# A gating stage whose first product is split into seven half-size products, and whose layer norm is applied behind the mixing

## The chip, the core and the metric

The program runs on one core of a Trainium2 chip. The core has a matrix engine (PE, whose weight loads are listed apart as PEld), a vector engine (DVE), a scalar engine (ACT), a third elementwise engine (POOL) and a sequencer (SP) that here only starts transfers. Each engine takes its instructions strictly in the order of its own list, and a wait at the head of a list holds back everything behind it. Transfers are started by SP or by POOL; only those of POOL add to what already stands at their target. The metric is the device time of one execution in microseconds (us), the median of several runs of one kernel.

## The reference

Two decoder layers work on 512 tokens of width 1024. Each layer has a mixer and an MLP, and each is fed by an RMS norm that is shifted and scaled by vectors made from a conditioning vector. Layer 0 mixes by pooling; layer 1 mixes by the gating stage, which this document is about:

```python
def layernorm(x, g, b):
    mu = jnp.mean(x, axis=-1, keepdims=True)
    xc = x - mu
    var = jnp.mean(xc * xc, axis=-1, keepdims=True)
    return xc * lax.rsqrt(var + LN_EPS) * g + b

def sgu_mixer(h, w_in, ln_g, ln_b, w_s, b_s, w_out):      # h: 1, 512, 1024
    z = jax.nn.gelu(h @ w_in, approximate=False)          # w_in: 1024, 2048
    u, v = jnp.split(z, 2, axis=-1)                       # the u half and the v half
    v = layernorm(v, ln_g, ln_b)
    v = v.reshape(B_, 4, 128, 8, 128)                     # chunks of 128 tokens, 8 heads of 128 channels
    ws = jnp.where(tril, w_s, 0)                          # w_s: 8, 128, 128
    mixed = jnp.einsum('hts,bnshc->bnthc', ws, v) + b_s.T[None, None, :, :, None]
    return (u * mixed.reshape(B_, S_, 1024)) @ w_out
```

## The kernel before

Every large product is made three times over: both operands are split into a high part (a rounded copy, made by ACT, line 201: `wh`) and a low part (the difference, made by DVE, line 202: `wl`), and `mm3` (line 214) adds low x high, high x low and high x high in PSUM. Activations have the same two parts: `hb` is the normed and modulated input, four tiles of two 128-channel blocks each, with hi and lo.

The first MLP ends with products in four chunks; the last of them, labelled `(3, 4)`, multiplies an activation tile `o` (hi by ACT line 680, lo by DVE line 681) with two weight tiles `bt`. Its 24 matmuls carry line 214 and the tile name `pm`; the rest of that MLP's matmuls are on line 976. Around it stands `normed(0, 1, 0)` (tokens 0 to 255) and, within the first v product, `normed(1, 1, 0)` (tokens 256 to 511): a reciprocal root on POOL (`rr`, line 281), a scaled copy of x (`xs`), 16 transposes on PE (`px`, line 1145), scale and shift (line 1152 on DVE, line 1150 on ACT), and the split into `hb`.

The gating stage before, in the order of PE:

1. The v product: two column halves x two halves of the tokens, 48 matmuls of 128x512 for each of these four pieces (`po<-wh,hb`), evicted by a GELU on ACT (line 1272).
2. The layer norm of v, on DVE: statistics (lines 1277, 1279), a small root on POOL, one pass for mean and root (line 1281), then two passes of 128x1024 for `ln_g` and `ln_b` per token tile (line 1283), whose rows were loaded to all partitions (`lnt`).
3. The u product by heads, `do_u(n)`: 8 input blocks x 3 = 24 matmuls of 128x512 for each of 8 heads (`po<-hb,wh`), GELU on ACT (line 1304). The weights lie in four plain loads of 1 MB (`ur`).
4. The mixing by heads, `do_mix(hd)`: four small products on PE (line 1312) into a PSUM bank, `b_s` added (line 1314), times u (line 1315), split for the last product (lines 1319, 1320). A string gives the order `u0 u1 u2 u3 m0 u4 m1 m2 u5 m3 m4 u6 m5 u7 m6 m7`.
5. The product with `w_out` (`po<-wh,gt`).

Between these, `ex` holds 24 small jobs that make columns of the conditioning vectors (`ada`, line 238 on DVE: one 512 KB load and one 128x1024 pass each) and one job, `spread_cols`, that turns a column into a row on all partitions by way of DRAM (`line`, `gainm`, `gb`).

PE's list is in program order. In this part of the program the lists of the other engines are made by the scheduler of the framework: it takes what is ready by its own estimate of time, and by the order of the program among what is ready. It, too, assigns buffers: the weight splits have five pairs, the pool of raw loads (`w4`) three buffers.

The MLPs already use the scheme that the change brings to u: `s_units` makes a quarter of the hidden layer by seven products of half the size, with sums of activations (the class `Sums`, whose passes are on lines 676, 705 and 706) and sums of weights. Sums of weights are made by transfers from POOL that add onto a tile (line 822).

## Time and profile before

| | |
|---|---|
| Time of the kernel, median of 3 runs | 836.05 us (835.79 to 836.57) |
| Time of the profiled execution | 835.0 us |
| Its span | 833.3 us |
| Instructions in it | 12670 |
| Mean granted TensorE clock | 0.998 |
| Transfers | 190.72 MB, 229 GB/s in the mean |

A span runs from the first to the last instruction that the profile holds; the time of the execution is 1.7 us more. Times within the program are us from the start of the span. A group row of the profile reads: line, engine, operation, output<-inputs by the program's names, shapes, x count, then busy us and mean ns of one. A timeline row reads: start, us, engine, line, operation, names, x count, and in square brackets how long the engine had been idle and what ended it. Matmuls overlap, so what one costs is read from the distance of starts and not from the length of one. DVE and ACT overlap a little too: a 128x1024 pass of DVE is listed with 1.22 us and the next one starts 1.14 us after it.

### The profile page before, as it was taken

To read this page: it belongs to the slowest core of one execution; us is meant where nothing else is said; L and a number is where in the kernel's file an instruction comes from. 1 tells how busy PE (TensorE), PEld (TensorE's weight loads), DVE (VectorE), ACT (ScalarE), POOL (GpSimd) and SP (SyncE) were. 2 spreads that over 40 slices of the span, in tenths; PEclk is the share of its full clock that TensorE was granted. 3 is DMA by queue.
4 is the path that set the end of the run, shared out by engine and by line. 5 is a ranking of instruction groups with operands and counts; after the bars stand their busy time and mean duration, and the time that the engine had idled before them with its cause. 6 is when DMAs were issued, how large, how long until landed. Compare 5 with 4: busy or idle time off the path is not lost.

```text
span 833.3 us, 12670 instructions
## 1 busy us (share of the span) xinstructions
PE 821.1 (99%) x4866; PEld 724.7 (87%) x4866; DVE 683.4 (82%) x882; ACT 506.3 (61%) x721; POOL 118.0 (14%) x140
## 2 busy tenths in 40 slices
PE   9999999999999999999999999999999999999996
PEld 6878899999888888888888888999999988888885
DVE  6999899998789868797898768795887678976887
ACT  3286777866756655676333237876776766565562
POOL 3010010000223200020110002100001032321000
PEclk9999999999999999999999999999999999999999
DMA  9999879999999989464757848865888799998502
GB/s 360 407 364 336 293 155 288 289 278 265 292 227 200 204 226 248 145 250 148 255 180 250 273 135 282 223 178 127 233 266 209 205 229 238 193 217 223 161 17 85
DMA packets 52227, 190.72 MB, mean 229 GB/s; under 512 B 5803, under 2 KB 5955, under 8 KB 51142
## 3 DMA queue, kind: packets, MB, share of 16 engines
q1 hardware_dynamic: 36944, 133.45, 44.3%
q0 software_dynamic: 14928, 56.12, 34.7%
q8 instruction: 38, 0.62, 0.3%
q10 hardware_dynamic: 294, 0.34, 0.1%
q14 instruction: 23, 0.19, 0.1%
HBM read 183.58 MB, written 6.30 MB: 228 GB/s over the span
## 4 chain that ended last, share of the span: by engine, by line
PE 82%; DVE 8%; DMA 5%; issue 2%; ACT 2%; POOL 0%; POOLq 0%; DVEq 0%; ACTq 0%
PE pm L976 28%; PE po L214 17%; PE b211q L214 3%; PE b315q L976 2%; PE b305q L976 2%; PE b201q L214 2%; PE b111q L214 2%; PE b205q L214 2%; DVE wl L202 2%; PE b101q L214 2%; PE b215q L214 2%; PE b301q L214 2%; DMA bt<-in_w 1%; DMA ada<-in_ada 1%; PE b011q L214 1%
## 5 line engine op out<-in xcount | busy, mean ns | idle before, releaser
L976 PE MATMUL pm<-wh,o 128*128 128x512 f32 x736 | 182.4, 390 | 0.5 <-DVE o L681 0.5
L976 PEld LDWEIGHTS pm<-wh,o 128*128 128x128 f32 x736 | 137.7, 188 | 29.5 <-DVE o L681 0.9
L976 PE MATMUL pm<-wl,o 128*128 128x512 f32 x368 | 98.4, 389 | 0.0
L201 ACT ACTIVATE wh<-bt 128x1024 fp32r<-128x1024 f32 x64 | 66.9, 1057 | 44.9 <-PE pm L976 33.7
L202 DVE TENSOR_TENSOR wl<-bt,wh 128x1024 fp32r<-128x1024 f32 x64 | 77.5, 1219 | 14.6 <-ACT wh L201 14.6
L976 PEld LDWEIGHTS pm<-wl,o 128*128 128x128 f32 x368 | 69.1, 188 | 14.4
L238 DVE SCALAR_TENSOR_TENSOR ada<-ada,cb 128x1024 f32<-128x1024 f32 x56 | 68.0, 1218 | 11.3 <-DMA ada<-in_ada 11.1
L681 DVE TENSOR_TENSOR o<-g,o 128x1024 fp32r<-128x1024 f32 x56 | 68.2, 1218 | 6.2 <-ACT o L680 6.2
L680 ACT ACTIVATE o<-g 128x1024 fp32r<-128x1024 f32 x56 | 58.6, 1048 | 10.1 <-PE pm L976 7.3
L214 PE MATMUL po<-hb,wh 128*128 128x512 f32 x208 | 64.1, 389 | 0.0
L201 ACT ACTIVATE wh<-raw 128x1024 fp32r<-128x1024 f32 x35 | 37.0, 1058 | 33.6 <-PE pm L976 13.5
L201 ACT ACTIVATE wh<-b 128x1024 fp32r<-128x1024 f32 x32 | 34.0, 1062 | 37.6 <-PE pm L976 31.4
L955 POOL DMA_DIRECT2D bt<-in_w x48 | 41.8, 906 | 104.9 <-DVE wl L202 104.8
L202 DVE TENSOR_TENSOR wl<-b,wh 128x1024 fp32r<-128x1024 f32 x32 | 39.2, 1224 | 21.3 <-ACT wh L201 21.3
L202 DVE TENSOR_TENSOR wl<-raw,wh 128x1024 fp32r<-128x1024 f32 x35 | 42.5, 1220 | 12.8 <-ACT wh L201 12.7
L214 PEld LDWEIGHTS po<-hb,wh 128*128 128x128 f32 x208 | 39.1, 188 | 7.9
L737 ACT ACTIVATE g<-g 128x512 f32<-128x512 f32 (+1 forms) x72 | 40.5, 579 | 1.1
L214 PE MATMUL po<-hb,wl 128*128 128x512 f32 x104 | 40.9, 393 | 0.0
L214 PE MATMUL po<-wh,gt 128*128 128x512 f32 x128 | 40.0, 391 | 0.0
L214 PE MATMUL po<-wh,hb 128*128 128x512 f32 x128 | 39.9, 390 | 0.0
L214 PEld LDWEIGHTS po<-wh,gt 128*128 128x128 f32 x128 | 24.0, 188 | 5.2 <-DVE gt L1320 0.2
L214 PEld LDWEIGHTS po<-wh,hb 128*128 128x128 f32 x128 | 24.0, 188 | 5.1
(469 smaller groups left out, 2096.6 us busy)
## 6 DMA issues: line engine op xcount, KB each, us to landing
ada<-in_ada SPq DMA_DIRECT2D x74, 512.0 KB, 5.2
bt<-in_w POOLq DMA_DIRECT2D x48, 512.0 KB, 10.1
bt<-in_w SPq DMA_DIRECT2D x16, 512.0 KB, 6.4
raw<-in_w SPq DMA_DIRECT2D x16, 512.0 KB, 6.9
b<-in_w SPq DMA_DIRECT2D x16, 512.0 KB, 4.8
b<-in_w POOLq DMA_DIRECT2D x16, 512.0 KB, 10.2
wh<-in_ada SPq DMA_DIRECT2D x8, 512.0 KB, 9.4
wl<-in_ada SPq DMA_DIRECT2D x8, 512.0 KB, 9.9
```

The costliest lines, as they stand in the source:

```text
L201: A.activation(h[:, c], r[:, c], AF.Copy)
L202: V.tensor_tensor(l[:, c], r[:, c], f32(h[:, c]), ALU.subtract)
L214: T.matmul(o[:, c], a, b[:, c], start=first and q == 0 and not c.start, stop=last and q == 2 and c.stop is None, **kw)
L238: keep(V.scalar_tensor_tensor(r, r, 1.0, cb, ALU.mult, ALU.mult, accum_out=pmv[i, b][:, j : j + 1]))
L680: A.activation(o[0], a, AF.Copy)
L681: V.tensor_tensor(o[1], a, f32(o[0]), ALU.subtract)
L737: A.activation(t, t, AF.Square)
L955: G.dma_start(r, piece(c, *nxt, q), accum_op=ALU.add)
L976: T.matmul(banks[hf], o[a][:, 2 * q + p, hf], w[q][b][:, S * p : S * p + S], start=start and q + n + p == 0, stop=stop and q + n + p == 4, ...
```

## The change

The u half of the first product is no longer made by heads but by two groups `j` of 512 channels. A group has four weight blocks of 512 x 256 (`w_u[j, r, n]`, r the half of the inputs, n the half of the columns), and seven products of 24 matmuls of 128x256. Products 1, 5, 6 and 4 use one weight tile (`ua[:, j]`) to which POOL's transfers add a further block each time the tile has been split; products 3 and 7 use `ub`, product 2 a raw load. The activation side needs sums of the normed input, so `normed` now keeps it in full precision (`h32`, in the slots S4 and S6) instead of in a two-buffer scratch tile (`tt`). Products 1, 6, 7, 4 add up in one PSUM bank, 5 and 3 in a second, 2 in a third that starts as a copy of the first.

The layer norm keeps only mean and root ahead of the mixing, in one pass on ACT. `ln_g` multiplies the mixed result (a number per partition, since channels lie on partitions there). For `ln_b` the sums over the rows of the masked `w_s` are made from a second load of it (`nat`), spread over the partitions, multiplied by `ln_b` and added to `b_s` (`row_sums`).

The order string, the places of the `ex` jobs and the order in which the last product takes its heads change as well.

```diff
-POPS = (3, 3, 3, 2, 2, 1, 1, 1)
...
+            h32[:] = [slot(t, [P, 4, S], "h32") for t in ("S4", "S6")]
...
-            tt = h32[k // 4][:, k % 4 : k % 4 + 2, c] if i and n else sm.tile([P, 2, 256], F32, name="tt", tag="tmp", bufs=2)
+            tt = h32[k // 4][:, k % 4 : k % 4 + 2, c] if i else sm.tile([P, 2, 256], F32, name="tt", tag="tmp", bufs=2)
...
+    lnc = sm.tile([P, LINE], F32, name="lnc", tag="lnc", bufs=1)
+    nc.sync.dma_start(lnc[:, 0 : 2 * HEADS], lnp)
+    rc = lnc[:, 2 * HEADS : 3 * HEADS]
+    ua, ub = (slot(t, [P, 2, D], "ur") for t in ("S5", "S7"))
+
+    def u_add(t, j, r, n):
+        G.dma_start(t, w_u[j, r, n], accum_op=ALU.add)
...
+    ALLU = [(0, m) for m in (1, 5, 2, 6, 3, 7)] + [(1, 1), (0, 4)] + [(1, m) for m in (5, 2, 6, 3, 7, 4)]
+    def u_prep(j, m):
+        if m == 2:
+            t = raw4(w_u[j, 1, 0])
+        else:
+            t = ub[:, m // 7] if m in (3, 7) else ua[:, j]
+        wu[j, m] = split(t, 1, RESET if m == 1 else UNDER)
+        if m in CHAIN_U:
+            u_add(t, j, *CHAIN_U[m])
+        elif j == 0 and m == 3:
+            nc.sync.dma_start(t, w_u[1, 1, 1])
+        elif j == 0 and m == 7:
+            nc.sync.dma_start(t, w_u[1, 0, 1])
+            u_add(t, 1, 1, 1)
+    CHAIN_U = {1: (0, 1), 5: (1, 1), 6: (1, 0)}
...
+        if m in (1, 5):
+            banks[j] = four[j] if m == 1 else bank(f"u{j}{m}q")
...
+        for f in range(2):
+            for k in range(4):
+                mm3(po[:, f], cut(wv, ALL, k, slice(P * f, P * f + P)), us_.of[m](k), m in (1, 5) and f + k == 0, m in (4, 3, 2) and f + k == 4, skip_group_check=True)
+        r, n = TAKES[m]
+        with tc.high_priority():
+            if m == 1:
+                WU[j] = seeded(full_u, f"u{j}2q", w[0])
+                A.activation(WU[j], XU[j], AF.Copy)
+                return
+            t = u_tile(j, n)[:, :, 256 * r : 256 * r + 256]
+            if m in (5, 6):
+                A.activation(t, po, AF.Copy)
+            elif m in (2, 4):
+                A.activation(t, po, AF.Gelu)
+            else:
+                V.tensor_tensor(t, *((po, t) if m == 3 else (t, po)), ALU.subtract)
+                A.activation(t, t, AF.Gelu)
...
+    def do_mix(hd):
+        po = mixed[hd] = four[(2, 3, 2, 3, 3, 2, 0, 2)[hd]]
...
+        V.scalar_tensor_tensor(o, o, lnc[:, hd : hd + 1], b, ALU.mult, ALU.add)
+        finish(hd)
+
+    def row_sums():
+        for hd in range(HEADS):
+            w = nat[:, P * hd : P * hd + P]
+            A.activation(w, w, AF.Copy, accum_out=rc[:, hd : hd + 1])
+        spread_cols(rc, "rows")
+        for hd in range(HEADS):
+            V.scalar_tensor_tensor(wb[1][:, hd], gbs[0][:, P * hd : P * hd + P], lnc[:, HEADS + hd : HEADS + hd + 1], wb[1][:, hd], ALU.mult, ALU.add)
...
-        V.tensor_scalar(v, v, ag[:, 0:1], r, ALU.subtract, ALU.mult)
-        for n, op in ((0, ALU.mult), (1, ALU.add)):
-            V.tensor_tensor(v, v, lnt[n].rearrange("p (a b) -> p a b", a=2), op)
+        V.scalar_tensor_tensor(m, ag[:, 0:1], -1.0, r, ALU.mult, ALU.mult)
+        A.activation(v, v, AF.Identity, bias=m, scale=r)
...
-    for op in "u0 u1 u2 u3 m0 u4 m1 m2 u5 m3 m4 u6 m5 u7 m6 m7".split():
+    for op in "u u u u m2 u m3 u u m0 m1 u u u m6 u m7 u u m4 u".split():
```

`finish(hd)`, called when both the mixing and u of a head are there, multiplies the two out of the PSUM bank and splits the product. In the lists that follow a number behind a name tells buffers apart, and the waits are those on DVE, ACT (Activation), PE, transfers of SP (DMAHW) and transfers of POOL (DMASW).

**At the end of the first MLP, on DVE.** `o_3531` (now `o_3529`) is the activation tile of the MLP's last product, its weight splits are `wl_3535` and `wl_3539` (now `wl_3533` and `wl_3537`), and the rows of `tt` or `h32` and `hb` are `normed(0, 1, 0)`. Before:

```order
L1152 TENSOR_SCALAR tt_3487<-px_3482,scl10_92,mods1_89 128x256
L1152 TENSOR_SCALAR tt_3497<-px_3492,scl10_92,mods1_89 128x256
L681 TENSOR_TENSOR o_3531<-g_1778,o_3531 128x1024
L202 TENSOR_TENSOR wl_3535<-bt_2496,wh_3534 128x1024
L681 TENSOR_TENSOR hb_3478<-tt_3487,hb_3478 128x2x256
L681 TENSOR_TENSOR hb_3479<-tt_3497,hb_3479 128x2x256
```

Now, from the fourth of the four scale-and-shift rows on:

```order
L1151 TENSOR_SCALAR h32_3479<-px_3511,scl10_92,mods1_89 128x256
L1080 TENSOR_TENSOR tmp_3520<-y_2775,gb_2697 128x512
L679 TENSOR_TENSOR hb_3480<-h32_3478,hb_3480 128x2x256
L1081 TENSOR_TENSOR x1_3298<-x1_3298,tmp_3520 128x512
L1080 TENSOR_TENSOR tmp_3525<-y_2775,gb_2697 128x512
L679 TENSOR_TENSOR hb_3481<-h32_3478,hb_3481 128x2x256
L679 TENSOR_TENSOR hb_3482<-h32_3479,hb_3482 128x2x256
L1081 TENSOR_TENSOR x1_3298<-x1_3298,tmp_3525 128x512
L679 TENSOR_TENSOR hb_3483<-h32_3479,hb_3483 128x2x256
L679 TENSOR_TENSOR o_3529<-g_1778,o_3529 128x1024
L200 TENSOR_TENSOR wl_3533<-bt_2496,wh_3532 128x1024
L200 TENSOR_TENSOR wl_3537<-bt_2497,wh_3536 128x1024
```

The low part of the MLP's last operand stood behind two scale-and-shift rows; it now stands behind four of them and eight passes of 128x512.

**In the u product, on ACT.** Before, the high parts of u's weights (`wh<-ur`) and the GELUs, with waits on plain loads:

```order
L201 ACTIVATE wh_4064<-ur_4062 128x1024 [waits DMAHW0_49,DVE_49]
L1304 ACTIVATE u_3963<-po_3982 128x512 [waits PE_49]
L201 ACTIVATE wh_4110<-ur_4062 128x1024 [waits DVE_49]
L1304 ACTIVATE u_3963<-po_4024 128x512 [waits PE_49]
L201 ACTIVATE wh_4161<-ur_4159 128x1024 [waits DMAHW1_49,DVE_49]
```

Now, with `wh_4093` the weights of product (0, 6), `wh_4125` those of (0, 3), `v_3601` the layer norm's pass over the last two token tiles, and `u02q` the PSUM bank in which product (0, 2) adds up:

```order
L199 ACTIVATE wh_4093<-ur_3598 128x1024 [waits DMASW4_49]
L199 ACTIVATE wh_4125<-ur_3599 128x1024
L1366 ACTIVATE v_3601<-v_3601,lnc_3596,rr_4031 128x1024 [waits DVE_49,Activation_49]
L1308 ACTIVATE u02q_4090<-po_4062 128x512 [waits PE_49]
L1366 ACTIVATE v_3601<-v_3601,lnc_3596,rr_4042 128x1024 [waits DVE_49,Activation_49]
```

The copy into `u02q`, without which product (0, 2) can't start, stands three rows behind a split that waits for a transfer of POOL.

**At the mixing, on DVE.** Before, around the mixing of heads 0 and 1:

```order
L1314 TENSOR_TENSOR po_4149<-po_4149,wsbs_3603 128x512 [waits PE_49]
L1315 TENSOR_TENSOR u_3963<-po_4149,u_3963 128x512 [waits DVE_49]
L202 TENSOR_TENSOR wl_4364<-raw_4361,wh_4363 128x1024 [waits DMAHW0_49,Activation_49]
L1320 TENSOR_TENSOR gt_4156<-u_3963,gt_4156 128x512 [waits Activation_49]
L1314 TENSOR_TENSOR po_4200<-po_4200,wsbs_3603 128x512 [waits PE_49]
```

Now, with `wl_4198` the weights of product (1, 1), `wl_4275` of (1, 5), `wl_4358` of (1, 6), and `po_4064` and `po_4065` the banks of heads 2 and 3, then of heads 0 and 1:

```order
L200 TENSOR_TENSOR wl_4198<-ur_3598,wh_4197 128x1024 [waits PE_49,Activation_49]
L200 TENSOR_TENSOR wl_4238<-ur_3598,wh_4237 128x1024 [waits DMASW7_49,PE_49,Activation_49]
L1345 SCALAR_TENSOR_TENSOR po_4064<-po_4064,lnc_3596,wsbs_3603 128x512 [waits PE_49]
L200 TENSOR_TENSOR wl_4275<-ur_3598,wh_4274 128x1024 [waits DMASW0_49,Activation_49]
L1316 TENSOR_TENSOR u_4123<-u05q_4098,u_4123 128x2x256 [waits PE_49]
L1345 SCALAR_TENSOR_TENSOR po_4065<-po_4065,lnc_3596,wsbs_3603 128x512 [waits PE_49]
L200 TENSOR_TENSOR wl_4322<-raw_4319,wh_4321 128x1024 [waits DMAHW4_49,Activation_49]
L1316 TENSOR_TENSOR u_4123<-u_4123,po_4062 128x2x256 [waits PE_49]
L200 TENSOR_TENSOR wl_4358<-ur_3598,wh_4357 128x1024 [waits DMASW2_49,DVE_49,Activation_49]
L1329 TENSOR_TENSOR u_4123<-po_4064,u_4123 128x512 [waits Activation_49]
```

The multiplication that frees the bank of head 2 for head 0 (the last row) stands behind the split of (1, 6), which waits for a transfer of POOL that can start only when (1, 5) has been split, and that one waits in the same way for (1, 1).

More of the change, by code (lines that the diff above doesn't have):

```diff
@@ L1255, in decoder_kernel @@
-    nc.sync.dma_start(wb[0], wsT)
-    nc.sync.dma_start(wb[1], bs.rearrange("(o a b) -> o a b", o=1, a=HEADS).to_broadcast([P, HEADS, P]))
-    G.affine_select(
-        out=wb[0], in_=wb[0], compare_op=ALU.is_ge, fill=0.0, base=0, pattern=[[0, HEADS], [1, P]], channel_multiplier=-1
-    )
+    ex = [lambda: spread_cols(mods[1][:, c_g(0, 0) : c_g(0, 0) + KD], "gainm")]
+    ex += [lambda q=q: ada_tile(1, q, ada1[8 + q], get4) for q in range(25, 40)]
+    ex[1:1] = [lambda: ada_tile(1, 24, ada1[32], lambda: slot("T00", [P, D], "ada"))]
@@ new lines, in finish @@
+    def finish(hd):
+        got[hd] = got.get(hd, 0) + 1
+        if got[hd] < 2:
+            return
+        u = u_tile(hd // 4, hd % 4 // 2)[:, hd % 2]
+        V.tensor_tensor(u, mixed[hd], u, ALU.mult)
+        if hd // 2 not in gt2:
+            gt2[hd // 2] = slot(("S4", "S6", "S5", "S7")[hd // 2], [P, 2, 2, S], "gt", F32R)
+        h, l = gt2[hd // 2][:, hd % 2, 0], gt2[hd // 2][:, hd % 2, 1]
+        A.activation(h, u, AF.Copy)
+        V.tensor_tensor(l, u, f32(h), ALU.subtract)
+        gt[hd] = h, l
@@ L1323, in decoder_kernel @@
[L1323 to L1324 removed]
+            if (ch, hf) == (0, 0):
+                nc.sync.dma_start(wb[0], wsT)
+                G.affine_select(
+                    out=wb[0], in_=wb[0], compare_op=ALU.is_ge, fill=0.0, base=0, pattern=[[0, HEADS], [1, P]], channel_multiplier=-1
+                )
+                for j in range(2):
+                    nc.sync.dma_start(ua[:, j], w_u[j, 0, 0])
+                us_.step(0)
+                pops(2)
+            elif (ch, hf) == (0, 1):
+                row_sums()
+                nc.sync.dma_start(ub[:, 0], w_u[0, 1, 1])
+                nc.sync.dma_start(ub[:, 1], w_u[0, 0, 1])
+                u_add(ub[:, 1], 0, 1, 1)
+                us_.step(1)
+                us_.step(2)
+                pops(3)
+            elif (ch, hf) == (1, 0):
+                u_prep(0, 1)
+                for t in range(2):
+                    layer_norm(t)
+                pops(3)
@@ new lines, in decoder_kernel @@
+    for m in (5, 2):
+        u_prep(0, m)
+    for t in (2, 3):
+        layer_norm(t)
+    us_.step(3)
+    pops(2)
+    four[:] = [bank("po", xz) for _ in range(4)]
+    at = 0
+    for op in "u u u u m2 u m3 u u m0 m1 u u u m6 u m7 u u m4 u".split():
+        if op != "u":
+            do_mix(int(op[1]))
+            continue
+        if at + 2 < len(ALLU) and ALLU[at + 2] not in wu:
+            u_prep(*ALLU[at + 2])
+        u_run(*ALLU[at])
+        if at in (2, 4, 6, 8, 10):
+            pops(1)
+        at += 1
```

119 lines of the change are left out of this document (58 added, 61 removed).

## The prediction

> **What bounds the kernel now.** I read the page first: the busy shares, then the chain that ended last.
>
> ```profile
> PE 821.1 (99%) x4866; PEld 724.7 (87%) x4866; DVE 683.4 (82%) x882; ACT 506.3 (61%) x721; POOL 118.0 (14%) x140
> PE 82%; DVE 8%; DMA 5%; issue 2%; ACT 2%; POOL 0%; POOLq 0%; DVEq 0%; ACTq 0%
> ```
>
> PE is the bound, with 12 us of idle time in 833. So time can be won only by taking work from PE, and whatever makes PE wait is lost in full. The same chain from 360 to 530 us, in order of time, gives what PE's pieces cost around the change:
>
> ```profile
> 361.73 5.46 PE pm L976 x24
> 367.19 5.44 PE pm L214 x24
> 372.63 8.17 PE po L214 x36
> 380.80 1.75 PE px L1145 x16
> 382.55 51.72 PE po L214 x228
> ...
> 439.86 0.89 PE po L1312 x8
> 440.75 5.46 PE po L214 x24
> ...
> 468.81 39.53 PE po L214 x174
> ...
> 514.20 2.83 PE b001q L214 x24
> 517.03 2.83 PE b011q L214 x24
> 519.85 0.23 PE b012q L134
> 520.09 2.73 PE b002q L214 x24
> ```
>
> It holds PE alone: no other engine ends a wait of PE between 360 and 530. A 128x512 matmul costs 5.46 / 24 = 0.227 us, a product of 24 half-size ones 2.73 to 2.83 (I take 2.8), filling a bank 0.23, the mixing of one head 0.89. The busy time by stretches (PE, PEld, DVE, ACT, POOL, then clock, share of the transfer engines, GB/s) tells how near DVE is to being a second bound:
>
> ```profile
> 418.00:425.00 7.00, 7.00 (x32) 5.82 (x31) 7.00 (x11) 3.19 (x4) 0.55 (x1) 1.00 0.43 152
> 425.00:435.00 10.00, 10.00 (x46) 8.17 (x45) 9.57 (x14) 2.24 (x5) 2.37 (x2) 1.00 0.47 160
> ```
>
> Where u begins DVE has no room at all; ACT and the transfers have.
>
> **What it takes off PE.** Eight u products of 5.46 (43.7) become fourteen of 2.8 (39.2), one bank fill (0.23) and one more transpose of a column (0.11, `pb` beside it costs that before): 39.5. That is -4.2; at 2.73 and 2.83 apiece it is between -5.1 and -3.7. The mixing stays.
>
> **What it puts on the others.** On DVE 12 passes of the norm go (four of 0.73, eight of 1.14: -12.0); six more splits, four sums and three low parts of 128x1024 (13 x 1.14), two low parts and four subtractions of 128x512 (6 x 0.60) and eight small passes (0.2 each, between 0.15 and 0.45 of the 128x1 and 128x256 forms) come: +20.0. Net +8.0 on an engine that was full at 418. On ACT about 20 us come; its 2 to 3 busy us in 10 there hide them, but not where one stands ahead of something urgent. The weights of u are read twice (4 MB more, `nat` 0.5, the norm's rows 1 MB less); transfer engines that are half idle hide 3.5 MB, which uncovered cost 9 us at 400 GB/s. What decides is therefore order: I follow the lists along the three places shown with the change.
>
> *The hand-over from the MLP.* DVE before:
>
> ```profile
> 361.17 0.99 DVE L1152 TENSOR_SCALAR tt<-px,scl,mods 128x256 f32<-128x256 f32 x2
> 362.07 1.21 DVE L681 TENSOR_TENSOR o<-g,o 128x1024 fp32r<-128x1024 f32 x1
> 363.21 1.21 DVE L202 TENSOR_TENSOR wl<-bt,wh 128x1024 fp32r<-128x1024 f32 x1
> 364.34 1.28 DVE L681 TENSOR_TENSOR hb<-tt,hb 128x512 fp32r<-128x512 f32 x2
> 365.55 0.99 DVE L1152 TENSOR_SCALAR tt<-px,scl,mods 128x256 f32<-128x256 f32 x2
> ```
>
> Starts are 1.14 apart for 128x1024, 0.60 for 128x512, 0.45 for 128x256. The two-buffer `tt` made the list return to `o` after two scale-and-shift rows. Now four of these (1.8) and eight 128x512 passes (4.8) come first: `o` begins at 361.17 + 6.6 = 367.8, ends 368.9, its first weight split 370.1, the second 371.2. PE is there at 367.19, and its second matmul needs the first split: it ends at 370.1 + 23 x 0.227 = 375.3 and not at 372.63. **+2.7.**
>
> Then POOL, whose list now has the selection of `nat` ahead of the root for the second `normed`:
>
> ```profile
> 370.29 4.22 POOL L1257 TENSOR_SCALAR_AFFINE_SELECT wsbs<-wsbs 128x1024 f32<-128x1024 f32 x1 [13.78 <-DMA wsbs<-in_wsT]
> 377.25 1.60 POOL L281 TENSOR_TENSOR rr<-rv,mhalf 128x2 f32<-128x2 f32 x1 [2.74 <-DVE rv L1110]
> 379.08 1.15 ACT L1133 ACTIVATE xs<-x,r 128x1024 f32<-128x1024 f32 x1 [2.30 <-DVE r L1112]
> raw<-in_w_v SPq DMA_DIRECT2D x8, 512.0 KB, 5.0
> ada<-in_ada SPq DMA_DIRECT2D x19, 512.0 KB, 4.3
> DMA to landing us min/median/max: 3.2/4.3/7.8
> ```
>
> `nat` needs the buffer of the second weight load of v, free when DVE has split it (371.2 + two splits = 373.5); like v's weights it lands 5.0 later (378.5), is selected (382.7), then come root 1.6, copy 0.2, `xs` 1.15: 385.7. PE is there at 375.3 + 8.17 = 383.5. **+2.2** (1.0 to 3.4). After 16 transposes and 12 matmuls PE wants the new `hb` at 390.2. On DVE three columns now stand ahead of it; the third may be loaded only when the first is used (386.5) and lands 4.3 later (the last row is that load's spread), so it ends at 391.9 and `hb` at 392.5. **+2.3** (1.1 to 4).
>
> *Product (0, 2).* Count from E, the end of the third of v's four pieces. PE then has 10.9 (48 matmuls), (0, 1), the fill and (0, 5): 16.7 us of work. The rows for the lists:
>
> ```profile
> 435.35 0.59 POOL L263 DMA_DIRECT2D gainm<-line  x1 [6.93 <-ACT line L261]
> 438.21 0.57 POOL L265 DMA_DIRECT2D gb<-gainm  x1 [2.27 <-DMA gainm<-line]
> gb<-gainm POOLq DMA_DIRECT2D x1, 512.0 KB, 6.5
> L201 ACT ACTIVATE wh<-ur 128x1024 fp32r<-128x1024 f32 x8 | 8.5, 1059 | 5.5 <-PE po L214 3.8 <-DVE v L1281 1.7
> L1314 DVE TENSOR_TENSOR po<-po,wsbs 128x512 f32<-128x512 f32 x8 | 5.5, 689 | 0.0
> DMA to landing us min/median/max: 5.2/6.7/10.3
> ```
>
> DVE waits for the spread row sums (the line is out at E - 9.5, the second transfer starts 2.9 later and takes 6.5: E - 0.1), makes eight small passes and a column (E + 2.7), then the statistics with two roots on POOL (E + 7.7), three columns (E + 11.1) and the split of (0, 5): E + 12.3. Only then may POOL add the next block. The last row is the landing of such adding transfers (line 822): I take 6.7. The split of (0, 6) on ACT starts at E + 19.0; behind it stand a second split, a pass of the norm and the copy that (0, 2) needs, 1.0 + 1.0 + 1.1 + 0.5: E + 22.6. **+5.9**: PE stands idle with the weights of (0, 2) split long before.
>
> *Mixing of head 0.* From that copy (C), ACT and DVE bring the split of (1, 1) by C + 4.7 (1.1 + 1.0 + 0.5 + 1.0 + 1.1); add 6.7, split of (1, 5) 2.1; add 6.7, split of (1, 6) 2.1; one multiplication 0.6: C + 22.9. PE has five products and two mixings, 15.8. **+7.1.** The bank is needed by head 0 and by nothing later than that; behind the split on DVE wait the mixing's own passes, behind the split's high part on ACT the GELUs. All later weights are then ready: from here PE has 24 us of work and one add of 6.7 in its way.
>
> *The clock.* At the end of the program PE stops at 825:
>
> ```profile
> 824.00:826.00 2.00, 1.22 (x11) 1.01 (x9) 1.52 (x6) 1.54 (x5) 0.54 (x1) 1.00 0.02 4
> 828.00:830.00 2.00, 0.00 (x0) 0.00 (x0) 0.75 (x1) 0.72 (x1) 0.00 (x1) 0.98 0.52 199
> 830.00:833.00 3.00, 0.00 (x0) 0.00 (x0) 0.00 (x0) 0.00 (x0) 0.00 (x0) 0.50 0.35 130
> 1.12 3.78 PE L350 MATMUL pc<-ones 128*128 128x128 f32 x16 [1.12 <-DVE edge L315]
> ```
>
> The granted clock halves some 5 us later. The last row is PE's start: 16 records of 128x128 take 0.236 each, where the mixing's take 0.89 / 8 = 0.111, so at least 3.8 us went by at half speed. A gap over 5 us then costs some 1.9. After (0, 2) this is swallowed by the wait that follows (its chain doesn't hang on PE); after head 0's it counts: **+1.9** (0 to 3.8). [...]
>
> In the last product the low part of head 5, now mixed within it, comes behind two columns, by the same count 0.7 late (0 to 1.5).
>
> **The sum**: 2.7 + 2.2 + 2.3 + 5.9 + 7.1 + 1.9 + 0.7 - 4.2 = +18.6. The profiled execution took 835.0 (span 833.3): 853.6. It was 1.05 below the median, so 854.6 for the median. The adds are the loosest term. Their lower bound is the fastest plain load, 3.2, the upper 10.3; they come once in the first wait (2.4 to 9.5) and twice in the second (0.1 to 14.3). All low ends give +1.6 (838), all high ones +35 (871).
>
> **Rivals.**
>
> *The adds are as quick as plain loads*, 3.2 to 4.3: the waits become 2.4 to 3.5 and 0.1 to 2.3, no gap reaches 5 us, and 7.2 + 3.0 + 1.2 + 0.7 - 4.2 = +7.9: **844**. For it: the transfer engines are half idle there. Against it: none of line 822 landed in under 5.2, and half took over 6.7. [...]
>
> *The adds are slow*, 10.3: 7.2 + 9.5 + 14.3 + 1.9 + 0.7 - 4.2 = +29.4: **865**. For it: the maximum of the row, and the columns' loads beside them.
>
> *PE stays the bound and keeps its gain.* If every piece is there when PE comes, only -4.2 is left: **831.9**, faster. It decides at the first place: `o` would have to be split by 367.2, so DVE would have to begin the 6.6 us ahead of it by 359.5, while the transposes it reads end at 361.7. For it: PE waited for none of these engines before, and DVE's mean room (122 of 143 us busy) takes 8 us more. It asks that each of three waits be hidden, so 11%.
>
> *No change* needs the waits to come to about 4: the hand-over's 7.2 and nothing else gives +3.7, already outside 0.2%. 3%.
>
> **How the numbers follow.** The forecast, slower by the three waits (847 to 862): 50%. Quick adds (838 to 847): 20%. Slow adds (862 to 872): 16%. Faster 11%, same 3%. Faster by over 0.2% (1.7 us, what a measurement here can tell from no change): 0.11; same 0.03; slower 0.86. The range leaves out the gain, no change and the upper half of the slow adds: 840 to 865.
>
> **What would show it.** Right: PE's idle groups name DVE `o` for some 2.7 us at the start of the MLP's last product; the root of the second `normed` follows a second selection directly; PE waits some 6 us for ACT `u02q` and some 7 us for DVE `u` at the mixing, behind `wl<-ur` and adding transfers of 6 to 7 us; DVE gains 8 us. The half-size products cost 2.8. Wrong: no PE wait over 1 us in the stage; adds landing in 3 us; or the copy of `u02q` done before (0, 5) ends.

## The result, and the profile after

The changed kernel takes **859.38 us** (median of 6 runs, 857.69 to 863.73), the kernel before on the same chip 835.92 (6 runs, 833.5 to 836.97): a ratio of 1.0295, 95% interval 1.0264 to 1.0326. It is slower by 23.5 us; predicted were 18.6, and a time of 854.6 in a range of 840 to 865. Line numbers below the change are two lower than before (L214 is now L212); in the experiments they differ by a few more.

The profiled execution took 863.73 us (span 862.0), the slowest of the six. Its page, busy shares and shares of the chain that ended last:

```profile
PE 827.6 (96%) x5012; PEld 735.6 (85%) x5012; DVE 693.7 (80%) x901; ACT 525.7 (61%) x759; POOL 121.7 (14%) x151
PE 73%; DMA 12%; DVE 9%; ACT 3%; issue 2%; POOL 1%; POOLq 0%; ACTq 0%; DVEq 0%; SPq 0%
```

PE had idled for 12 us of the span; now it is 34, and the chain leaves PE for a transfer or DVE in a fifth of the span. PE's waits by the engine that ended them (total us, times, longest), the six largest of the stage:

```profile
PE po L1343 <- DVE u L1329: 7.7, 1, 7.7
PE u02q L212 <- ACT u02q L1308: 5.5, 1, 5.5
PE po L212 <- DVE hb L679: 4.4, 1, 4.4
PE pm L212 <- DVE o L679: 2.1, 1, 2.1
PE po L212 <- DVE u L1316: 1.9, 1, 1.9
PE pm L212 <- DVE wl L200: 0.7, 1, 0.7
```

Four of the six rows are waits that the prediction had named, and the `wl` row belongs to its first one. The `u L1316` row is new: the last u product, (1, 4), waits for a subtraction.

A single number for the whole program hides where the time goes, since one execution differs from the next by some 3 to 5 us elsewhere too (in the traces of this document the stage described next begins between 365.9 and 371.4 us). So I compare one **stage**: from the end of the first MLP's L974 products (367.19 before) to the first product of the second MLP (`b001q`). All stage numbers are read from PE's timeline of one execution each: the stage, the waits of PE in it, and what is left over PE's own work, which is 146.9 - 4.2 = 142.7 us by the kernel before and the saving. "changed again" is the control of the experiments, the changed kernel run once more beside them. A ratio is that of the mean times, to the kernel before on the same chip; the runs were made on several chips, so two rows are compared by their ratios first. Each stage is that of one execution: for the changed kernel the slowest of its runs, for "subtract first" the fastest (851.14).

| kernel | time, ratio [95%] | stage | waits | rest over 142.7 |
|---|---|---|---|---|
| before | 835.92 | 146.9 | 0 | (4.2) |
| changed | 859.38, 1.0295 [1.0264, 1.0326] | 176.6 | 22.5 | 11.4 |
| changed again | 860.33, 1.0282 [1.0246, 1.0317] | 172.4 | 22.4 | 7.3 |
| norm alone | 836.52, 1.0010 [0.9987, 1.0033] | 147.6 | 0.5 | (4.4) |
| PE kept busy | 864.22, 1.0335 [1.0309, 1.0361] | 174.2 | 13.7 | 6.7, and 94 x 0.118 = 11.1 of added work |
| multiply first | 859.75, 1.0264 [1.0220, 1.0309] | 169.5 | 18.5 | 8.3 |
| copy first | 861.52, 1.0288 [1.0228, 1.0348] | 175.2 | 22.7 | 9.8 |
| hand-over kept | 861.97, 1.0314 [1.0281, 1.0347] | 175.3 | 24.0 | 8.6 |
| plain transfers | 854.95, 1.0205 [1.0163, 1.0248] | 164.4 | 15.0 | 6.7 |
| order by hand | 885.80, 1.0583 [1.0548, 1.0617] | 199.6 | 41.1 | 15.8 |
| subtract first | 855.16, 1.0233 [1.0193, 1.0273] | 164.5 | 14.8 | 7.0 |
| order by hand 2 | 868.21, 1.0385 [1.0349, 1.0421] | 180.6 | 23.0 | 14.9 |
| plain, subtract first | 844.97, 1.0106 [1.0072, 1.0139] | 157.8 | 10.4 | 4.7 |
| no adding | 842.01, 1.0072 [1.0044, 1.0099] | 153.3 | 7.1 | 3.5 |

(In brackets: kernels that still have the 4.2 us of work.) The rest is mostly time at half clock: within the stretches of its stage that were granted half, PE worked 20.9 us in the changed kernel and 12.3 in the control, and half of that, 10.5 and 6.2, is what full clock would have saved by estimate. Stretches of the changed kernel (from:to, length, busy PE, PEld, DVE, ACT, POOL, granted clock, share of the transfer engines, GB/s), each behind a gap:

```profile
370.00:372.00 2.00, 1.50 (x4) 1.24 (x5) 2.00 (x3) 0.00 (x0) 0.00 (x0) 0.52 0.84 250
396.00:400.00 4.00, 4.00 (x11) 3.12 (x10) 4.00 (x7) 2.00 (x2) 0.00 (x0) 0.50 0.38 156
468.00:472.00 4.00, 4.00 (x20) 4.00 (x20) 2.90 (x5) 1.14 (x2) 0.15 (x1) 0.50 0.77 131
494.00:496.00 2.00, 2.00 (x11) 2.00 (x11) 2.00 (x4) 0.64 (x1) 0.00 (x0) 0.50 0.68 236
```

PE is busy in them, but for the half us of a gap in the first, and gets half its clock. In the second one 11 matmuls of 128x512 start in 4 us, where 17 or 18 fit at 0.227.

How the two large waits came about is seen in the chain of waits, in order of time (start, length, what):

```profile
428.57 9.90 DMA ur<-in_w_u
438.50 1.56 ACT wh L199 x2
...
441.63 0.48 ACT u02q L1308
...
447.21 8.35 DMA ur<-in_w_u
...
458.63 5.29 DMA ur<-in_w_u
464.02 1.06 ACT wh L199
465.11 1.22 DVE wl L200
466.33 0.61 DVE u L1329
466.94 0.04 issue
466.99 3.78 PE po L1343 x16
```

An adding transfer of 9.9 us, then the two high parts, the norm's pass and the copy `u02q` behind it; then two more adding transfers, and behind the second the split and the multiplication that frees the bank. That is the order which the lists had shown. The chain names only one cause of the first wait, though. The norm's pass needs numbers that DVE makes behind a column, and that column's load landed as late as the transfer:

```profile
438.70 1.23 DVE L236 SCALAR_TENSOR_TENSOR ada<-ada,cb 128x1024 f32<-128x1024 f32 x1 [5.25 <-DMA ada<-in_ada]
```

The numbers were ready at 440.1 and the second high part at 440.1 too, so a quicker transfer alone would not have removed this wait. The eight transfers themselves (L1254: POOL's time at each issue in ns, min/median/max, and the time to landing):

```profile
L1254 POOL DMA_DIRECT2D ur<-in_w_u x8: 862/882/1219, 384.1 to 467.3; - x8
DMA to landing us min/median/max: 5.3/7.5/9.9
```

### The profile page after: what moved, and what is told of

Its sections match the earlier page's. It is cut to its first block, busy times and chain, and to the rows that moved or that the text cites. A ratio compares the mean times of both kernels' runs of the same rounds, so it can differ in the third digit from the quotient of the medians.

```text
span 862.0 us, 13038 instructions
## 1 busy us (share of the span) xinstructions
PE 827.6 (96%) x5012; PEld 735.6 (85%) x5012; DVE 693.7 (80%) x901; ACT 525.7 (61%) x759; POOL 121.7 (14%) x151
## 4 chain that ended last, share of the span: by engine, by line
PE 73%; DMA 12%; DVE 9%; ACT 3%; issue 2%; POOL 1%; POOLq 0%; ACTq 0%; DVEq 0%; SPq 0%
PE pm L974 26%; PE po L212 10%; DMA ur<-in_w_u 4%; DVE wl L200 3%; PE b101q L212 3%; PE b111q L212 3%; PE b211q L212 3%; PE b201q L212 3%; DMA ada<-in_ada 3%; PE b305q L974 2%; PE b315q L974 2%; DMA bt<-in_w 2%; PE b115q L212 2%; PE b205q L212 2%; PE b301q L212 2%
## 5 line engine op out<-in xcount | busy, mean ns | idle before, releaser
L974 PE MATMUL pm<-wh,o 128*128 128x512 f32 x736 | 182.5, 390 | 0.8 <-DVE o L679 0.8
L974 PEld LDWEIGHTS pm<-wh,o 128*128 128x128 f32 x736 | 137.7, 188 | 29.9 <-DVE o L679 1.2
L974 PE MATMUL pm<-wl,o 128*128 128x512 f32 x368 | 98.4, 389 | 0.0
L200 DVE TENSOR_TENSOR wl<-bt,wh 128x1024 fp32r<-128x1024 f32 x64 | 77.5, 1219 | 15.0 <-ACT wh L199 14.9
L974 PEld LDWEIGHTS pm<-wl,o 128*128 128x128 f32 x368 | 69.1, 188 | 14.4
L678 ACT ACTIVATE o<-g 128x1024 fp32r<-128x1024 f32 x56 | 58.6, 1048 | 10.2 <-PE pm L974 7.4
L199 ACT ACTIVATE wh<-raw 128x1024 fp32r<-128x1024 f32 x37 | 39.1, 1057 | 30.9 <-PE pm L974 13.5
L200 DVE TENSOR_TENSOR wl<-raw,wh 128x1024 fp32r<-128x1024 f32 x37 | 44.9, 1221 | 11.5 <-ACT wh L199 11.5
L212 PE MATMUL po<-wh,hb 128*128 128x512 f32 x128 | 42.3, 409 | 4.4 <-DVE hb L679 4.4
L212 PE MATMUL po<-hb,wh 128*128 128x256 f32 (+1 forms) x176 | 43.7, 341 | 0.0
L212 PE MATMUL po<-wh,gt 128*128 128x512 f32 x128 | 40.4, 392 | 0.2 <-DVE gt L1334 0.2
L212 PEld LDWEIGHTS po<-wh,hb 128*128 128x128 f32 x128 | 25.4, 198 | 10.4 <-DVE hb L679 4.8
L212 PEld LDWEIGHTS po<-hb,wh 128*128 128x128 f32 x176 | 31.5, 201 | 3.1
L212 PE MATMUL po<-hb,wl 128*128 128x256 f32 (+1 forms) x88 | 30.4, 346 | 1.9 <-DVE u L1316 1.9
L1091 ACT ACTIVATE tmp<-x 128x512 f32<-128x512 f32 (+1 forms) x24 | 14.8, 618 | 26.0 <-DVE x L1081 21.9
## 6 DMA issues: line engine op xcount, KB each, us to landing
bt<-in_w POOLq DMA_DIRECT2D x48, 512.0 KB, 10.4
```

Source lines behind the costliest of these rows:

```text
L199: A.activation(h[:, c], r[:, c], AF.Copy)
L200: V.tensor_tensor(l[:, c], r[:, c], f32(h[:, c]), ALU.subtract)
L212: T.matmul(o[:, c], a, b[:, c], start=first and q == 0 and not c.start, stop=last and q == 2 and c.stop is None, **kw)
L678: A.activation(o[0], a, AF.Copy)
L974: T.matmul(banks[hf], o[a][:, 2 * q + p, hf], w[q][b][:, S * p : S * p + S], start=start and q + n + p == 0, stop=stop and q + n + p == 4, ...
L1091: A.activation(tmp, xt, AF.Square, scale=D**-0.5, accum_out=o)
```

## The experiments

The theory after the first look: three things stand between PE and its saving of 4.2 us, namely transfers that add and land late, lists that DVE and ACT work strictly in order with a late load ahead of something urgent, and the clock that gaps cost. The rival in most runs is that a wait taken away comes back at the next place, because the lists behind it are late as well.

**The layer norm's part alone**, on the kernel before: its channel vectors behind the mixing, u as it was.

```diff
...
-        V.tensor_scalar(v, v, ag[:, 0:1], r, ALU.subtract, ALU.mult)
-        for n, op in ((0, ALU.mult), (1, ALU.add)):
-            V.tensor_tensor(v, v, lnt[n].rearrange("p (a b) -> p a b", a=2), op)
+        m = lnc[:, 3 * HEADS + t : 3 * HEADS + t + 1]
+        V.scalar_tensor_tensor(m, ag[:, 0:1], -1.0, r, ALU.mult, ALU.mult)
+        A.activation(v, v, AF.Identity, bias=m, scale=r)
...
-        V.tensor_tensor(p4, p4, wb[1][:, hd, :].unsqueeze(1).to_broadcast([P, 4, P]), ALU.add)
+        V.scalar_tensor_tensor(p4, p4, lnc[:, hd : hd + 1], wb[1][:, hd, :].unsqueeze(1).to_broadcast([P, 4, P]), ALU.mult, ALU.add)
...
```

> Edit: of the change only the layer norm's part, in the kernel before: mean and root in one pass on ACT, ln_g behind the mixing, the row sums for ln_b; u stays by heads. Theory: PE's work is the same but for one transpose, DVE loses 12 us and gets 3 back, nothing it makes is late: within 1.5 us of the kernel before, and no wait of PE over 1 us between 360 and 530 us. So the loss is the u part's. Rival: the row sums (a column, two transfers, eight small passes) come late for the first mixing or push v's weights back, as in the changed kernel: 2 to 5 us slower than the kernel before.

836.52 us, ratio 1.0010 [0.9987, 1.0033]: no change that can be told. On its page DVE is less busy and PE is not moved:

```profile
PE 822.1 (99%) x4867; PEld 724.5 (87%) x4867; DVE 675.3 (81%) x882; ACT 512.6 (61%) x742; POOL 120.6 (14%) x143
```

DVE's 8 us less (683.4 before) are worth nothing while PE is the bound, and PE waits 0.5 us in the stage. So by itself the norm's part costs nothing, and the loss comes with the u part. That the two don't hinder each other is not shown: in the change the selection of `nat` and the norm's passes stand ahead of rows that PE waits for, and this run selects `nat` at another place.

**PE kept busy** with 40 and 54 matmuls of 128x256 into a bank not yet in use, ahead of product (0, 2) and of the mixing of head 0; their results are overwritten.

```diff
+        if (j, m) == (0, 2):
+            busy(four[1], 40)
...
+            if op == "m0":
+                early.append(bank("u15q"))
+                busy(early[0], 54)
```

> Edit: nothing is undone. 40 more half-size matmuls (4.5 us) into a bank that nobody reads stand on PE ahead of product (0, 2), and 54 (6.1 us) ahead of the mixing of head 0, so that PE works while it waits. Theory: beside the waits the change pays for the clock, which goes to half speed in or just after each wait; (0, 2) then takes 4.2 us in place of 2.8, the mixing of heads 0 and 1 3.4 in place of 1.7, and (0, 4) 3.8 in place of 2.8. With PE kept busy these three fall back to 2.8, 1.7 and 2.8, the waits themselves stay: 4 us faster than the changed kernel, and the granted clock stays at 1.0 from 433 to 485 us. Rival 1: the slow matmuls behind a wait come from something else (weights just written, transfers beside them): no gain, or 1 us lost where the added matmuls run over. Rival 2: only gaps of over 5 us matter, as the prediction had it: then 1.9 us, from the second place alone.

```profile
442.00:446.00 4.00, 3.31 (x29) 3.11 (x28) 3.59 (x8) 4.00 (x6) 0.89 (x1) 1.00 0.74 279
468.00:472.00 4.00, 3.57 (x31) 3.58 (x32) 3.65 (x6) 2.18 (x3) 0.86 (x1) 1.00 0.39 62
```

The clock stays at 1.00 behind both places, and product (0, 2) is back at 2.84 us from 4.24, the mixing of two heads at 1.80 from 3.43. So the slow products were the clock's and not, say, the weights'. The stage is 2.4 us shorter than in the changed kernel's first profile and 1.8 longer than in the control, the time no better (864.22): the waits that follow take up what the clock gives back (2.4 are left at the mixing, 3.3 at (1, 4)), and in that execution PE had come to the stage 2 to 3 us later, which the changed rows don't explain. As a remedy it failed, as a test of the cause it is clear.

**The multiplication first**: the split of (1, 6) is issued behind the multiplication of head 3 on DVE and the GELU of (0, 7) on ACT.

```diff
+        if (j, m) == (1, 6):
+            late_.enter_context(tc.issue_after(mults[3].ins))
+            late_.enter_context(tc.issue_after(gelus[0, 7].ins))
         wu[j, m] = split(t, 1, RESET if m == 1 else UNDER)
```

> Edit: the split of (1, 6) is listed behind the multiplications of heads 2 and 3 on DVE and behind the second GELU of group 0 on ACT; nothing else is moved by more than two rows. Theory: the mixing of head 0 waits for the bank that the multiplication of head 2 frees, and that one stands only behind the split, which waits for an adding transfer. With it ahead the wait of 7.7 us falls to 3 (the subtraction at 460.3, GELU, multiplication: 462.3 in place of 467.0), (1, 6) has its weights still before PE comes: 4.7 us faster than the changed kernel, up to 6.5 with a shorter time at half clock. Rival 1: the wait moves to product (1, 5) or (1, 6), whose weights come no earlier: 0 to 1 us faster, with a new wait of 4 us or more there. Rival 2: the bank is not what is waited for: no change.

PE's waits, and DVE's row in front of the one that is now the largest (in brackets how long DVE itself had waited, and for what):

```profile
PE po L212 <- DVE u L1321: 6.7, 1, 6.7
PE u02q L212 <- ACT u02q L1313: 4.9, 1, 4.9
PE po L1349 <- DVE u L1334: 0.9, 1, 0.9
```

```profile
487.00 1.23 DVE L236 SCALAR_TENSOR_TENSOR ada<-ada,cb 128x1024 f32<-128x1024 f32 x1 [5.87 <-DMA ada<-in_ada]
```

The wait at mixing head 0 fell from 7.7 (6.6 in the control) to 0.9: its cause was the split ahead of the multiplication. But 3.8 us of it came back at (1, 4): DVE sat 5.9 us before a column whose load (`ada`) had not landed, with the subtraction for PE right behind. The time is 859.75, not told from the control (three of the four runs took 859.6 to 859.9, one 852.9).

**The copy first**: the copy into `u02q` ahead of the splits of (0, 6) and (0, 3) and of the norm's passes on ACT.

```diff
+        with tc.issue_after(copied[0].ins) if (j, m) in ((0, 6), (0, 3)) else nullcontext():
+            wu[j, m] = split(t, 1, RESET if m == 1 else UNDER)
...
+        if at == 0:
+            with tc.issue_after(copied[0].ins):
+                for f in applied:
+                    f()
```

> Edit: the copy into the bank of product (0, 2) is listed on ACT ahead of the layer norm's passes over the last two token tiles and ahead of the splits of (0, 6) and (0, 3). The scheduler moves some columns on DVE as well. Theory: the wait of 5.5 us at (0, 2) goes, and PE comes 6.9 us sooner to (0, 6); but the split of (0, 6) hangs on its transfer and now stands behind the layer norm, so PE waits there for 4 to 5 us, and the mixing of head 0 still waits for the chain of transfers through (1, 1), (1, 5) and (1, 6). Waits are passed on: -2 to +1 us against the changed kernel. Rival: each wait stands by itself and its removal is won in full: 5.5 us, 6.9 with the clock.

```profile
PE po L212 <- DVE wl L200: 5.4, 1, 5.4
PE po L212 <- DVE u L1317: 5.2, 1, 5.2
PE po L1344 <- DVE u L1330: 3.3, 1, 3.3
```

```profile
438.28 1.23 DVE L236 SCALAR_TENSOR_TENSOR ada<-ada,cb 128x1024 f32<-128x1024 f32 x1 [5.68 <-DMA ada<-in_ada]
```

Product (0, 2) no longer waits at all, and PE stands 5.4 us one product further, at (0, 6). The adding transfer of its weights landed at 438.1, but ACT began their split only at 442.0: the norm's two passes stood ahead of it, and these waited for numbers that DVE makes behind the column of the last row, whose load landed late too. The waits sum to 22.7, as before (22.5), and the time is 861.52. So two chains end at this place almost together, the transfer and the norm behind a late column, and taking the copy out of the way of the one leaves the other.

**The hand-over kept**: the norm of the rows is held back until the MLP's last product has its operand, `nat` is loaded and selected later, and the columns go behind `hb`.

```diff
-    after(us, ("p", (1, 4)), ("x", lambda: normed(0, 1, 0, rr.pop)))
+    after(us, ("p", (1, 4)), ("w", ("p", (3, 4))), ("x", lambda: normed(0, 1, 0, rr.pop)))
...
-                pops(2)
+                with tc.issue_after(hbs[-1].ins):
+                    pops(2)
```

> Edit: the operand and weights of the MLP's last product are prepared in program order ahead of the first normed input; the second copy of the masked weights is loaded and selected after the first v piece, so that POOL has the root first; the two columns after that piece are listed behind the second normed input. Theory: all three waits of the hand-over (2.1, 0.7 and 4.4 us, with some 5 us at half clock behind them) go: the product after the last wait starts 12 us sooner. DVE has only 6 us of idle time in the 40 us of the hand-over and is full behind it, so the u product's preparation moves forward by 4 to 6 us, and the wait at (0, 2) grows by the rest: 5 to 7 us faster than the changed kernel. Rival 1: everything behind follows PE: 12 us faster. Rival 2: DVE's work sets the pace alone: 0 to 2 us faster, the whole gain given back at (0, 2).

```profile
PE po L1345 <- DVE u L1331: 8.7, 1, 8.7
PE po L212 <- DVE wl L200: 7.5, 3, 3.9
PE u02q L212 <- ACT u02q L1310: 4.3, 1, 4.3
```

The waits for `o` and `hb` (7.2 us) are gone. In their place PE waits 7.5 us for splits of v's weights, which now stand behind the passes that were held back, and the mixing of head 0 starts at 466.87, to a tenth where it started in the changed kernel (466.99). What PE won ahead of that point it spent waiting there, since what the mixing waits for came no earlier: 861.97, where 5 to 7 us of gain had been expected.

**Plain transfers**: the eight transfers of POOL overwrite instead of adding; the sums of weights are left out.

```diff
-        G.dma_start(t, w_u[j, r, n], accum_op=ALU.add)
+        G.dma_start(t, w_u[j, r, n])
```

> Edit: the eight transfers that add a block onto a weight tile of u now overwrite the tile; same queue, same bytes, every list is row for row the same (the sums of weights are left out, so u is another). Theory: it is the adding that makes them slow (5.3 to 9.9 us, median 7.5, in the changed kernel); plain ones land in 4 to 5 us, so the chain (1, 1), (1, 5), (1, 6) ahead of the mixing of head 0 is 4 us shorter, while the wait at (0, 2) keeps its other cause (the layer norm's numbers on DVE behind a column whose load is late) and loses 0 to 1 us: 4 to 5 us faster than the changed kernel. Rival 1: the queue or the busy transfer engines make them slow, not the adding: they land in 5 to 10 us as before, no change. Rival 2: both waits are set by the transfers alone: 8 us or more faster.

The same two rows of L1254, and the two waits that matter:

```profile
L1254 POOL DMA_DIRECT2D ur<-in_w_u x8: 527/529/613, 388.4 to 459.4; - x8
DMA to landing us min/median/max: 3.6/5.0/7.5
```

```profile
PE po L212 <- DVE u L1316: 4.3, 1, 4.3
PE po L1343 <- DVE u L1329: 2.2, 1, 2.2
```

With the sums they land in 5.3/7.5/9.9 (5.3/7.0/9.1 in the control). Bytes, queue and order are equal, so it is the adding that costs the 2 us or more. Mixing head 0, behind two of them, waits 4.4 us less than in the control; the time is 854.95, 5.4 less.

**The order by hand**: DVE's and ACT's lists of the stage written out, with 14 columns moved (in the string `u` are products, `p` the splits of their weights, `c` columns, `m` mixings).

```diff
+    OPS = "u01 p06 p03 L s u05 p07 c u02 s c p11 c u06 c p04 m2 u03 c m3 u07 u11 p15 p12 m0 m1 c u04 u15 c u12 p13 m6 p16 u16 g m7 p17 u13 u17 c m4 p14 u14"
...
+    hand_ = tc.manual_schedule(engines={mybir.EngineType.DVE, mybir.EngineType.Activation})
```

> Edit: the whole change, but from the first MLP's last product to the mixing the lists of DVE and ACT are written out by hand: the last product's operand ahead of the normed input, the second copy of the masked weights later, each weight split as soon as its buffers are free and never ahead of a pass that PE waits for sooner, 14 of the 24 columns moved behind the u product. Theory: PE's saving of 4.2 us is real and only the order of the lists turned it into a loss; with every chain of transfers begun early enough PE waits under 3 us in the stage: 831 to 837 us, between 4 us faster and 2 us slower than the kernel before. Rival 1: DVE's work (40 us of it in the 45 us of the v product) and the chains of three adding transfers are too long whatever the order: PE still waits 6 to 12 us in all and the time is 840 to 848. Rival 2: no better than the changed kernel, over 855.

```profile
PE po L212 <- DVE wl L200: 15.7, 4, 8.0
PE po L1348 <- DVE u L1334: 11.6, 1, 11.6
```

Much worse, 885.80. The seven u products ahead of the mixing of head 0 ran without a wait, but the columns that I had put between them arrived late (DVE stood 3.4 and 3.6 us before two of them), splits of later weights came behind them, and PE waited 7.0 us for the row sums, which stood behind other work on ACT. A second order tried to mend these places (w_v's first split ahead of the norm, row sums early, columns spread evenly, w_o's behind w_o's loads):

> A second order of DVE's and ACT's lists written by hand: w_v's first split ahead of the norm of the rows, row sums early on ACT, columns spread evenly and each behind its load, w_o's columns behind w_o's loads. Theory (the loss is the order of the lists): the waits of the first hand order at PE (15.7 us on the splits of w_v, 11.6 us on DVE's subtractions, 7.0 us on the row sums) fall to under 8 us together, time 838 to 848 us. Rival (DVE's 80% of the span is packed too tight in this stretch for any order): at least 15 us of waits stay in the stage, time 855 us or more.

```profile
PE po L214 <- DVE wl L202: 12.7, 6, 6.4
PE pb L259 <- ACT nat L1356: 4.1, 1, 4.1
```

868.21, with 23 us of waits, 12.7 us of them in six waits for splits and 4.0 at the mixing of head 0: the rival of that expectation. Two orders that fail don't show that none is good enough; they show that each place mended made another late. Whether DVE's list has room for all that the stage asks stays open.

**The subtractions first**: beside the multiplication ahead of (1, 6), the columns for w_o go behind the subtraction of (1, 7), so that no late load stands before a subtraction.

```diff
-                pops(1 + (dh == 1 and t == 0))
+                with tc.issue_after(subs[-1].ins):
+                    pops(1 + (dh == 1 and t == 0))
...
-        if at in (2, 4, 6, 8, 10):
+        if at in (2, 4, 6, 8, 12):
```

> Beside the multiplication ahead of the split of (1,6), the columns that DVE adds up for w_o (with loads that landed late) are issued behind the subtraction of (1,7), so that no column with a late load stands ahead of the subtractions for which (1,4) waits. Theory (each wait is DVE or ACT working its list in order, with a late load ahead of the urgent instruction): the wait of 6.7 us that stood at (1,4) with the multiplication first falls to at most 2, the wait at mixing head 0 stays under 1.5, the stage from the first MLP's last product to w_o is 9 to 11 us shorter than in the changed kernel, time 849 to 853 us. Rival (DVE has no room: the work put off is due before the next product anyway): another product of the same stretch or w_o waits by 5 us or more, time 857 to 861 us.

```profile
PE po L1351 <- DVE u L1336: 2.2, 1, 2.2
PE po L212 <- DVE u L1336: 1.8, 1, 1.8
```

Product (1, 4), which had waited 6.7 us, runs without a wait; the mixing waits 2.2, and the first product of w_o 1.8 for a multiplication, which stood behind a column whose load was 2.9 us late: the same pattern one place on. The stage is 12.1 us shorter than in the changed kernel and 7.9 than in the control; 9 to 11 had been expected. The time is 855.16, a little above the 849 to 853 of the theory and the best of the kernels with the new u product that compute its sums: two late rows moved together gain 4 to 5 us by the ratios, where one alone gained nothing that can be told. Against the first measurement of the changed kernel this is clear; the interval of the control just overlaps.

**The same order with plain transfers**, and **the same order without the eight transfers** at all; both leave out the sums of weights.

> The order of e8 with the eight transfers that add in flight made plain ones (the sums of weights are left out: each half-size product reads the second block alone). Theory (landing 2 us later and the order of the lists are two separate causes of waits in series): the two gains add, 5 us of the plain transfers and 6 to 9 of the order, time 845 to 849 us. Rival (both act on the same wait, at mixing head 0, so the gains overlap): time within 2 us of the better of the two alone, 850 to 855 us.

```profile
PE u02q L212 <- ACT u02q L1315: 5.5, 1, 5.5
```

> The order of e8 without the eight transfers that add (the sums of weights are left out: the splits use the block that stands in the tile), everything else the same: the half-size products, the splits, DVE's further additions. It bounds what any arrangement of the transfers could reach. Theory (the u part loses by waits, the saving of PE of 4.2 us is real): the waits at (0,2) and mixing head 0 go, since no split stands late ahead of the copy or the multiplication; left are some 5 us of waits before the products (the hand-over) and 2 to 3 of half clock, so the stage is about 150 us against 146.9 in the kernel before, time 836 to 841 us. Rival (the adds that DVE now makes cost more than the transfers' lateness): waits of 6 us or more stay at the subtractions or the mixing, time 843 us or more. Second rival (the saving outweighs what is left): 832 us or less.

```profile
PE pm L212 <- DVE o L679: 2.2, 1, 2.2
PE u02q L212 <- ACT u02q L1315: 2.1, 1, 2.1
PE po L212 <- DVE hb L679: 1.8, 1, 1.8
```

Plain ones (landing in 5.2 at the median): 844.97. That is 10.2 less than with sums, twice what they gave in the old order, and not an overlap: with the order mended, what the transfers give is no longer eaten at (1, 4), where PE no longer waits. Without any: 842.01 beside 836.76 before, ratio 1.0072. It lies between the theory's 836 to 841 and the rival's 843. By place the theory holds, since the mixing and the subtractions have no wait left, but (0, 2) kept 2.1 us that I had counted as gone. There the copy stands behind the norm's pass, and that one behind statistics, roots and columns.

So, taken away in this order, the loss of some 24 us splits into about 13 from the transfers (855.16 - 842.01; most of it from their adding, 10.2 by the plain ones), 4 to 5 from late loads ahead of the multiplication and the subtractions (ratio 1.0282 or 1.0295 against 1.0233), and 6 that stay with neither: the hand-over, (0, 2) and their clock cost more than the saving brings. In another order the shares are others, since plain transfers alone gave 5.4.

## Why the prediction was right, and where it was not

- **The saving** (-4.2) is real: half-size products start 2.72 to 2.83 us apart at full clock. No order tried here brought it as time, not even without the transfers (842.01).
- **The last product of the MLP** (+2.7): right. `o` began at 368.0 (367.8 predicted), PE waited 2.1 + 0.7 = 2.8.
- **The root behind the second selection and `hb` behind the columns** (+2.2, +2.3): right in sum, 4.4, but it stands at `hb` alone; in the control 1.1 at the transposes and 3.8 at `hb`. `xs` came when predicted (385.65 for 385.7). PE came later, because the clock had halved behind the gap before, and so didn't have to wait there; in the control the clock stayed full behind that gap, and PE waited.
- **Product (0, 2)** (+5.9): 5.5 (4.6 in the control), by luck, since two errors cancel. By the count from the third piece's end (10.9 ahead of (0, 1), which began at 430.56: 419.6) the add began at 428.6 and not at 419.6 + 12.3 = 431.9, and took 9.9 us, not 6.7. The second chain behind this wait, the norm's numbers behind a late column, was in no term. With the hand-over kept the splits of (0, 6) and (0, 3) were done at 436.0, and the copy still began only at 439.8, behind the norm's pass.
- **Mixing of head 0** (+7.1): 7.7 (6.6 in the control). The two adds took 8.35 + 5.29 = 13.6 (13.4 predicted). Multiplying first took the wait away, so the bank was its cause.
- **The last product** (+0.7): 0.2 (0.5 in the control).
- **Not foreseen**: the wait at (1, 4), 1.9 and 2.9. The step that failed is "all later weights are then ready": it looked at weights and transfers, and not at the subtractions on DVE's list nor at the load ahead of them.
- **The clock** (+1.9) is the term that was mis-sized: 6.2 to 10.5 by the estimate above, in a rest of 7.3 to 11.4. The step was that only a gap over 5 us halves the clock. In the trace gaps of 2.8 us (2.06, one matmul, 0.73) and even 1.9 us did it, with 1 to 3 us lost behind each gap that halved it; in the control the same 2.8 us, and one of 2.9, did not (the last section shows where they fell). That the time lost after (0, 2) is swallowed by the next wait was not refuted: with the hand-over kept, PE came earlier and the mixing of head 0 began when it had. I had read the bound from the end of the program, where the halving came 5 us after the last matmul, as if it were the shortest gap that matters.
- **DVE** gained 10.3 us of busy time (8 predicted).

The waits were predicted at 2.7 + 2.2 + 2.3 + 5.9 + 7.1 + 0.7 = 20.9 and came to 22.5 and 22.4. With the clock of the control, 22.4 + 7.3 - 4.2 = 25.5 for the stage, and 24.75 for the times: the error of the forecast, 5 to 6 us, is mostly the clock. That the waits agree in sum to 1.6 us is in part luck: (0, 2) came out by errors that cancel, and the wait at (1, 4) was in no term.

Three small readings of the working were off and change no conclusion: the low ends as listed give +2.2 and not +1.6, which is 838 all the same; DVE was busy 115 us in 143 us from 367.19 by its view, not 122; and ACT was busy 3.2 us in the 7 from 418, more than the 2 to 3 in 10 that were said. The 400 GB/s that stand beside the 3.5 MB are near the highest of the page's 40 slices before, 407.

**The rivals.** "Adds as quick as plain loads" was wrong twice: the adds took 7.0 to 7.5 at the median, and with plain transfers, which landed in 5.0, the time was 854.95, not 844, since other rows of the lists are late then. "Slow adds" was the case of one transfer (9.9), not of all. "PE keeps its gain" asked that three waits be hidden; none was.

## What to carry to other kernels

Where the bound engine had no wait, a saving on it is paid for by every row that has to come earlier on engines that work their lists in order: follow each list up to the instruction that the bound engine needs, and write down which late load or adding transfer stands ahead of it, for results and freed banks as well as for weights. Waits in series are passed on: here each late row that was moved alone gained nothing that could be told, two together 4 to 5 us, quicker transfers alone 5.4 us, and all of these 15 (844.97 against 860.33). A gap of the bound engine can also cost half clock behind it, here 1 to 3 us; gaps of 2.1 and 0.7 us at the end of the MLP did it in one execution of the changed kernel and not in the other, so two executions of one kernel differ by it.
